# Half of the first columns' products from x times the scale, with the norm and the shift put on the sums

## The chip, the core and the metric

The kernel runs on one NeuronCore of a Trainium2 chip. The metric is the device time of one execution, in microseconds. TensorE (PE in the profile; PEld is its weight load) multiplies, VectorE (DVE) and ScalarE (ACT) work elementwise, GpSimd (POOL) does a few small things, and SyncE (SP) issues the DMAs. Every engine runs its own instructions in the order in which they were written into its queue, and waits on semaphores for the others.

## The reference, cut to what matters

One layer of a diffusion backbone: 1024 tokens of width 1024, 256 context tokens, eight heads of 64, and a gated short convolution beside the attention.

```python
shift, scale, gate = adaln(c, w_ada, b_ada)            # silu(c) @ w_ada + b_ada
h  = rmsnorm(x, norm_g) * (1 + scale) + shift
hc = rmsnorm(ctx, norm_g) * (1 + scale_c) + shift_c
q, k, v, za, u, bg, cg, zc = split(h @ w_in)
kc, vc = split(hc @ w_in[:, 512:1536])
attn = neighbourhood_attention(q, k, v, kc, vc, rpb) * silu(za)
conv = bg * conv3(cg * u) * silu(zc)
x_new = x + gate * (concat(attn, conv) @ w_out)
```

For one feature k and one token t, h is x[t,k] * r[t] * s[k] + b[k]: r is the token's reciprocal root mean square, s is norm_g * (1 + scale), b the shift. So h @ w = r[t] * sum_k (x[t,k] s[k]) w[k] + sum_k b[k] w[k]. The first term without r needs no root mean square, and the second is one number for each column of w.

## The kernel before, in words

Everything is computed with features on the 128 partitions and tokens along the free axis: h lies transposed, as eight k tiles of 128 features by 1024 tokens. For fp32 accuracy each operand is split into a high part (fp32r) and the rest, and each product is three matmuls: high by high, high by low, low by high. `hh[k]` and `hl[k]` are the two parts of h; "half 0" and "half 1" are tokens 0 to 511 and 512 to 1023.

**The first stage** loads everything that h needs and, while that arrives, already multiplies h by the first 384 columns of the convolution (128 columns each of u, bg, cg). Its order is written out by hand: `LOADS` and `STEPS` are lists of words, and `do` runs for each word the function that `does` names. A word writes its instructions into its engine's queue, so the order of the words is the order on each engine. The words, with k the feature tile and h the half:

- `xN`: load the token tile N of x (128 tokens, 512 KB); `thk`: load half h of the transposed x, tile k (256 KB); `sk`: load the slab of the modulation weights for k (1 MB); `ck`, `qk`: a chunk of 384 weight columns (192 KB), for the convolution and for the first projection pair; `n0`, `n1`: context tiles; `e`: transposed context; `g`: the rotary tables.
- `sqN`: ACT squares and sums a token tile; `rootG`: DVE adds epsilon and POOL takes the power -0.5, for a group of tiles (0 and 1 are the halves, 2 is the context); `RtG`: PE turns and spreads the result over the partitions, into a bank `tr`; `RG`: ACT copies it to `spread_r`.
- `prk`: PE multiplies the conditioning vector by slab k (64 small matmuls, into a bank `tr`); `tpk`: DVE turns the rows; `abk`: DVE makes s[k] and b[k] from them.
- `uhk`: DVE makes x * s * r; `hihk`: ACT adds b and writes the high part; `lohk`: DVE writes the low part.
- `chk`, `clk` (and `qhk`, `qlk`): the weight chunk's high part on ACT and the low part on DVE.
- `fchki`: three matmuls, one for each of u, cg, bg, of part i (0 high by high, 1 the low weights, 2 the low h), into the six banks `acc0[column][half]`.
- `TN`, `v0k`: for half 0 and k of 0 and 1, PE turns x itself and DVE normalizes it; `warm`, `fill`: matmuls that only keep PE busy.
- `conv0`: one step of the convolution's first group (`conv_group(0, done)`): copies the sums of u, multiplies by the sums of cg. The taps and the product with bg follow behind the list.
- `rgN`: DVE makes the rotary tables.

**PSUM** has eight banks. In this stage six are `acc0` and two `tr`. Behind it two pools take the eight: `psm` with tags O, U and C, `pss` with tag S, two banks each. A tile of a new pool waits until the old tiles in its bank have been read.

**The second stage** runs over n = 0 to 31: four head pairs by eight token tiles. `proj_tile` multiplies 128 tokens of h by 384 columns (24 matmuls) into a bank whose tag goes round by t % 4. At n = 0, behind the first tile's products, `CONTEXT` makes the context's h (`Hi`, `Lo`: DVE scales, ACT adds the shift and rounds, DVE takes the rest). At n = 2 `ctx_products` multiplies it, 32 matmuls, which PE does in order behind tile 2. Each tile is then normalized by head, rotated, turned and stored; `head_scale` and `normed` read its bank. Beside that stand the convolution's gate unit, sums of blocks of the output weights (`add_blocks`, n = 6 to 25) and **the gate row**: `gate.load(kt)` loads 512 KB of weights, `gate.add(kt)` does two DVE additions a tile, `split` and `sum` end it; the result is loaded into `ab[:, :, 0]`, which the end of the kernel multiplies by.

The third stage is the attention with more units of products as filler, the fourth the output projection.

Of the kernel before, what the change touches and what calls it, by code (L numbers as in the profile page):

```python
# [34 lines left out]

LOADS = "x0 x1 x2 x3 s0 c0 s1 c1 x4 x5 x6 x7 t10 t11 s2 t02 t12 c2"
STEPS = [
# [11 lines left out]
]  # L49
# [6 lines left out]
def body(tc, es, x, xb, xt, cb_, ct, w_mod, w_gate, b_ada, w_grp, w_col, q_g, k_g, bias, w_out, vecs, cst, out):  # L56
# [352 lines left out]
    def conv_group(i, done=None):  # L409
# [6 lines left out]
        def keep(half, ps):  # L416
            ub[half] = cvp.tile([P, 512], F32, name="ub", tag="ub", bufs=2)
            act.copy(ub[half], ps)

# [122 lines left out]
    wpp = wps.enter_context(sbuf("wpp"))  # L542
    cxp = wps.enter_context(sbuf("cxp"))
    xs = ExitStack()
    xp = xs.enter_context(sbuf("xp"))
# [4 lines left out]
    def tr():  # L550
        return ps0.tile([P, 512], F32, name="tr", tag="tr", bufs=2)

# [3 lines left out]
    def load_x(t):  # L556
        if t < 4:
            if t % 2 == 0:
                pair.append(place(6 + t // 2, [P, 2, D], F32, "xn"))
            xn[t] = pair[t // 2][:, t % 2]  # L560
        else:
            xn[t] = xp.tile([P, D], F32, name="xn", tag="xn", bufs=4)[:]
        sp.dma_start(xn[t], xb[t * P:(t + 1) * P] if t < NB else cb_[(t - NB) * P:(t - NB + 1) * P])

    def load_t(half, k):
        xh[half, k] = xp.tile([P, 512], F32, name="xh", tag="xh", bufs=6)
        sp.dma_start(xh[half, k], xt[k, :, half * 512:(half + 1) * 512])
# [10 lines left out]
    for u, half in (0, 0), (2, 0), (0, 1), (2, 1), (1, 0), (1, 1):  # L578
        acc0[u][half] = ps0.tile([P, 512], F32, name=f"acc{u}{half}", tag=f"acc{u}{half}")

    sums = [xp.tile([P, 4], F32, name=f"sums{i}") for i in range(3)]
    spread_r = [xp.tile([P, 512], F32, name=f"rs{i}") for i in range(2)] + [cxp.tile([P, L], F32, name="rs2")]

    def square(t):

        sqj = xp.tile([P, D], BF16, name="sqj", tag="sqj", bufs=1)
        act.activation(sqj, xn[t], AF.Square, scale=1.0 / 32, accum_out=sums[t // 4][:, t % 4:t % 4 + 1])

# [41 lines left out]
    def early(k):  # L630
        return acc0[(0, 2)[k]][1]

# [10 lines left out]
    def scale_early(k):  # L643

        hw = bmp.tile([P, 3 * 384], F32, name="hw", tag="bt", bufs=2)
        scaled[0, k] = hw[:, :512]
        dve.tensor_scalar(scaled[0, k], scaled["v", k], ab[:, k, 1:2], ab[:, k, 0:1], ALU.mult, ALU.add)

    def shift_high(key, hi, k, w):
        if ("v", k) in scaled and key == (0, k):  # L650
            act.activation(hi, scaled["v", k], AF.Identity, bias=ab[:, k, 0:1], scale=ab[:, k, 1:2])
            return
        act.activation(hi, scaled[key], AF.Identity, bias=ab[:, k, 2 * w:2 * w + 1])

    def shift_low(key, lo, hi, k, w):
        if ("v", k) in scaled and key == (0, k):
            scaled.pop(("v", k))
            dve.tensor_tensor(lo, scaled.pop(key), hi.bitcast(F32), ALU.subtract)
            return
        dve.scalar_tensor_tensor(lo, scaled.pop(key), ab[:, k, 2 * w:2 * w + 1], hi.bitcast(F32), ALU.add, ALU.subtract)  # L660

    def half_of(v, half):
        return v[:, half * 512:(half + 1) * 512]

    def first_columns(half, k, i):

        wh, wl = chunks[k][:2]
        for u in (0, 2, 1):
            uc = slice(u * P, (u + 1) * P)
            pe.matmul(acc0[u][half], (wl if i == 1 else wh)[:, uc], half_of(hl[k] if i == 2 else hh[k], half),  # L670
                      start=k == 0 and i == 0, stop=k == KT - 1 and i == 2)

    def cast_chunk(raws, k):
        raw = raws[k][:].rearrange("p a b -> p (a b)")
        w = wpp.tile([P, 2, 384], F32R, name="w", tag="w", bufs=12)
        act.copy(w[:, 0], raw)
        raws[k] = raw, w

    def rest_of_chunk(raws, k):
        raw, w = raws[k]  # L680
        dve.tensor_tensor(w[:, 1], raw, w[:, 0].bitcast(F32), ALU.subtract)
        raws[k] = w[:, 0], w[:, 1], w[:, :, P:384]

# [15 lines left out]
    def gains(i):  # L699

        rw, gqk = tables[0]
        if i == 0:
# [6 lines left out]
        if i == 3:  # L709
            sp.dma_start(rope_d, tables[1][:].rearrange("p n b k d -> p (n b k d)"))  # L710
# [13 lines left out]
    def keep_clock(n, late=False):  # L724

        v = zeros[:].rearrange("p (o n) -> p o n", o=1).broadcast_to([P, 4, P]) if late else warm
        ps = acc0[1][1][:].rearrange("p (a n) -> p a n", a=4) if late else acc0[1][1]
        for _ in range(n):
            pe.matmul(ps, zeros if late else warm[:, :P], v, start=True, stop=True)
# [7 lines left out]
        "Rt": lambda g: copies.update({g: spread_rows(g)}), "R": lambda g: copies[g](),  # L737
        "pr": lambda k: products(k), "tp": lambda k: turned_rows(k), "ab": lambda k: modulation(k),
        "ch": lambda k: cast_chunk(chunks, k), "cl": lambda k: rest_of_chunk(chunks, k),
# [52 lines left out]
    def bank(name, tag):  # L792
        return (pss if tag == "S" else psm).tile([P, 512], F32, name=name, tag=tag, bufs=2)
# [357 lines left out]
    for n in range(NT + 3):  # L1151
# [21 lines left out]
        if 6 <= n < 26 and blocks[1] == 0:  # L1173
            load_blocks(blocks[0])
        if n == 16:
            sp.dma_start(ab[:, :, 0], g_d.rearrange("o (t p) -> p (o t)", p=P))
# [424 lines left out]
```

## Time and profile before

| | us |
|---|---|
| median of 3 runs (lowest, highest) | 587.03 (586.88, 587.1) |
| the profiled execution | 587.34 |
| its span, first to last instruction | 585.6 |
| PE busy in it | 577.2 (99%) |
| DVE busy in it | 438.6 (75%) |
| ACT busy in it | 282.0 (48%) |

The time of an execution is a little more than the span, since it also holds what lies around the instructions. A row of the timeline gives start, length, engine, line, operation, the tile written and those read, shapes, and xcount where instructions of one kind were merged; in brackets stands the engine's idle time before it and what ended it. Nearly all lines are L71, the helper that records the instructions in order, so the tiles' names tell the places: `acc` are the first columns' sums, `pacc` a projection tile, `cacc` the context products, `h` the parts of h, `hw` the scaled x before them, `hc` the context's h, `w` weight chunks, `rs` the spread roots, `rg` rotary tables, `cu` and `cv` the convolution, `gacc` the gate row.

### The profile page before, as it was taken

To read this page: it belongs to the slowest core of one execution; us is meant where nothing else is said; L and a number is where in the kernel's file an instruction comes from. 1 tells how busy PE (TensorE), PEld (TensorE's weight loads), DVE (VectorE), ACT (ScalarE), POOL (GpSimd) and SP (SyncE) were. 2 spreads that over 40 slices of the span, in tenths; PEclk is the share of its full clock that TensorE was granted. 3 is DMA by queue.
4 is the path that set the end of the run, shared out by engine and by line. 5 is a ranking of instruction groups with operands and counts; after the bars stand their busy time and mean duration, and the time that the engine had idled before them with its cause. 6 is when DMAs were issued, how large, how long until landed. Compare 5 with 4: busy or idle time off the path is not lost.

```text
span 585.6 us, 9903 instructions
## 1 busy us (share of the span) xinstructions
PE 577.2 (99%) x3531; PEld 483.3 (83%) x3532; DVE 438.6 (75%) x890; ACT 282.0 (48%) x653; POOL 57.4 (10%) x82
## 2 busy tenths in 40 slices
PE   8899999999999999999999999999999999999997
PEld 4578999999999999988878787878787867888886
DVE  1578879656846746367998788998979887999952
ACT  5636355336525545433463474466535646643420
POOL 1001033123223232100000000000000001100000
PEclk9999999999999999999999999999999999999999
DMA  8997666845756695686253646564758273773532
GB/s 323 410 415 278 220 229 211 283 166 194 267 189 213 224 341 205 226 297 219 73 209 120 243 140 229 182 216 155 254 187 257 80 263 96 248 252 89 199 125 91
DMA packets 66679, 126.14 MB, mean 215 GB/s; under 512 B 8714, under 2 KB 27650, under 8 KB 64325
## 3 DMA queue, kind: packets, MB, share of 16 engines
q1 hardware_dynamic: 66244, 124.70, 60.8%
q0 software_dynamic: 384, 0.81, 0.6%
q8 instruction: 28, 0.46, 0.3%
q14 instruction: 23, 0.18, 0.1%
HBM read 92.38 MB, written 33.10 MB: 214 GB/s over the span
## 4 chain that ended last, share of the span: by engine, by line
PE 91%; DMA 5%; DVE 2%; ACT 1%; SPq 0%; issue 0%; POOL 0%; DVEq 0%; ACTq 0%
PE pu L71 29%; PE pacc L71 23%; PE pout L71 13%; PE acc L71 5%; PE po L71 5%; PE cacc L71 4%; PE pss L71 3%; DMA xn<-in_xb 3%; PE pc L71 3%; PE pmx L71 2%; PE trA L71 1%; PE tr L71 1%; DMA y_d<-tb 1%; PE ptot L71 1%; PE trB L71 1%; DVE sb L71 0%
## 5 line engine op out<-in xcount | busy, mean ns | idle before, releaser
L71 PE MATMUL pu<-h,uh 128*128 128x512 f32 x544 | 174.4, 402 | 0.0
L71 PE MATMUL pacc<-w,h 128*128 128x384 f32 x768 | 138.5, 337 | 0.0
L71 PEld LDWEIGHTS pacc<-w,h 128*128 128x128 f32 x768 | 132.8, 188 | 0.2
L71 PEld LDWEIGHTS pu<-h,uh 128*128 128x128 f32 x544 | 97.3, 188 | 18.4 <-issue 1.2
L71 PE MATMUL pu<-h,ul 128*128 128x512 f32 x272 | 106.5, 391 | 0.0
L71 PE MATMUL pout<-right,left 128*128 128x512 f32 (+2 forms) x348 | 77.0, 383 | 0.0
L71 PEld LDWEIGHTS pout<-right,left 128*128 128x128 f32 x348 | 64.4, 188 | 12.7
L71 PEld LDWEIGHTS pu<-h,ul 128*128 128x128 f32 x272 | 51.1, 188 | 11.5
L71 POOL TENSOR_TENSOR ss<-ss,few 128x4 f32<-128x4 f32 (+1 forms) x40 | 41.4, 1035 | 127.0 <-DVE ss L71 126.7
L71 ACT COPY sc<-pc 128x512 f32<-128x512 f32 x32 | 18.7, 587 | 44.6 <-PE pc L71 44.6
L71 PE MATMUL acc<-h,w 128*128 128x512 f32 x144 | 35.3, 397 | 1.4 <-ACT h L71 1.4
L71 ACT ACTIVATE sc<-sc 128x512 f32<-128x512 f32 x32 | 20.3, 633 | 33.7 <-DVE sc L71 33.6
L71 ACT ACTIVATE sq<-pacc 128x256 f32<-128x256 f32 x32 | 12.3, 386 | 47.4 <-PE pacc L71 46.7
L71 DVE TENSOR_TENSOR sum<-sum,sb 128x372 f32<-128x372 f32 (+2 forms) x64 | 31.1, 485 | 2.7
L71 PEld LDWEIGHTS acc<-h,w 128*128 128x128 f32 x144 | 26.3, 188 | 7.8 <-ACT h L71 2.1
L71 DVE SCALAR_TENSOR_TENSOR m<-pout,ab,m 128x512 f32<-128x512 f32 (+2 forms) x34 | 22.9, 717 | 13.0 <-PE pout L71 12.9
L71 ACT ACTIVATE qn<-pacc,ss 128x64 f32<-128x64 f32 x128 | 30.0, 330 | 4.8 <-PE trA L71 2.5
L71 DVE TENSOR_TENSOR mx<-mx,sb 128x372 f32<-128x372 f32 (+2 forms) x64 | 30.8, 481 | 1.4
L71 DVE TENSOR_REDUCE ss<-sq 128x4 f32<-128x260 f32 (+1 forms) x40 | 15.7, 393 | 21.5 <-ACT sq L71 21.5
L71 DVE TENSOR_TENSOR ul<-uraw,uh 128x512 fp32r<-128x512 f32 x34 | 23.1, 685 | 10.0 <-ACT uh L71 10.0
L71 DVE TENSOR_TENSOR sb<-pss,bt 128x192 f32<-128x192 f32 (+3 forms) x48 | 27.5, 600 | 2.3 <-PE pss L71 2.2
L71 DVE TENSOR_TENSOR qs<-trA,qs 128x512 fp32r<-128x512 f32 x16 | 11.1, 691 | 21.2 <-ACT qs L71 20.2
(142 smaller groups left out, 862.8 us busy)
## 6 DMA issues: line engine op xcount, KB each, us to landing
uraw<-in_w_col SPq DMA_DIRECT2D x34, 256.0 KB, 3.8
slab<-in_w_mod SPq DMA_DIRECT2D x8, 1024.0 KB, 9.0
q_d<-qs SPq DMA_DIRECT2D x32, 256.0 KB, 4.0
k_s<-k_d SPq DMA_DIRECT2D x8, 1024.0 KB, 6.9
q_s<-q_d SPq DMA_DIRECT2D x16, 512.0 KB, 3.9
wr<-in_w_grp SPq DMA_DIRECT2D x40, 192.0 KB, 5.0
bt<-in_rpb SPq DMA_DIRECT2D x8, 564.0 KB, 6.8
xn<-in_xb SPq DMA_DIRECT2D x8, 512.0 KB
```

The source lines that it names most:

```text
L71: i = emit(*a, **kw)
```

## The change

Half 1's first columns no longer take the true h. Word `p1k` (ACT) writes the high part of x * s, `m1k` (DVE) the low part, both into half 1 of `hh[k]` and `hl[k]`; the `fc1ki` multiply these. The shift goes through PE on its own: `shk` (ACT, in place of DVE's second operation in `ab`) writes b[k] into a table `b32` of 32 columns, `wbk` multiplies it by the raw weight chunk (four fp32 matmuls of 96 columns, in the four column groups of a new bank `shifted`), and `wt` (DVE) turns the sum. Behind the last product `rp0` to `rp2` (DVE) multiply the three banks of half 1 by the spread roots, and in `conv_group` ACT adds the shift's column to each of the three, one of them in the copy that was there. The true h of half 1, which the projection tiles from t = 4 on read, is made afterwards by the same `u1k`, `hi1k`, `lo1k`, over the plain parts.

The words stand in a new order: slabs and transposed x of half 1 come first, token tiles of x later; the `fc` words begin with half 1. `tr` has one bank in place of two, the buffers of token tiles go from four to two, those of the transposed x from six shared to three and eight. `proj_tile`'s tags go S, S, O, O. The gate row's loads, additions and sum, and the load of the result, come eight tiles later.

```diff
-LOADS = "x0 x1 x2 x3 s0 c0 s1 c1 x4 x5 x6 x7 t10 t11 s2 t02 t12 c2"
+LOADS = "s0 t10 c0 x0 s1 t11 c1 x2 x3 x1 s2 c2 t12 t02"
 STEPS = [
...
+    "ch0 pr0 s3 t13 c3 t03 t14 c4 t04 tp0 ab0 p10 cl0 sh0 sq0 fc101 fc100 m10 fc102 pr1 s4 x4 x5 T0 ch1 wb0 tp1",
+    "ab1 cl1 p11 sh1 m11 fill2 fc110 sq2 sq3 fc111 fc112 sq1 root0 wb1 T3 ch2 T2 fill5 pr2 s5 tp2 ab2 cl2 sh2 p12",
+    "m12 T1 more Rt0 wb2 R0 fc120 fc121 v00 fc122 hi00 v01 u00 hi01 pr3 lo00 u01 lo01 u02 t05 t15 c5 fc000 fc002",
+    "fc010 tp3 hi02 ab3 fc001 ch3 fc012 p13 fc011 lo02 cl3 fc020 sh3 u03 fc022 hi03 ch4 fc021 m13 fc132 pr4 cl4",
+    "tp4 fc131 sq4 x6 ab4 lo03 fc130 u04 sh4 p14 fc031 fc140 sq5 x7 t16 s6 c6 t06 s7 t17 c7 t07 hi04 fc032 lo04",
+    "ch5 fc141 sq6 fc030 cl5 pr5 fc042 tp5 fc041 fc040 sh5 ab5 wb3 q0 p15 u05 fc151 hi05 sq7 m14 ch6 fc050 root1",
+    "fc150 lo05 m15 fc142 cl6 pr6 tp6 ab6 fc152 sh6 p16 u06 wb5 wb4 q1 q2 g0 n0 n1 m16 hi06 fc051 fc052 ch7 lo06",
+    "pr7 fc162 qh0 qh1 cl7 tp7 fc160 ql0 ab7 qh2 Rt1 fc161 ql1 p17 u07 sh7 wb6 q3 R1 hi07 ql2 u10 fc060 sq8 fc171",
+    "wb7 q4 q5 q7 q6 e0 e1 e2 e3 lo07 u11 fc062 hi10 m17 fc061 fc072 qh3 fc170 sq9 wt ql3 fc071 lo10 qh4 fc172",
+    "hi11 u12 ql4 rp0 root2 qh5 fc070 qh6 ql6 qh7 ql5 ql7 hi12 lo12 lo11 conv0 rp1 u13 u14 hi13 hi14 rg3 lo13 u15",
+    "lo14 hi15 u16 rg0 lo15 rp2 u17 rg2 rg1 hi17 conv0 lo17 Rt2 hi16 R2 lo16",
...
-        ps = bank("pacc", "OOSS"[t % 4])
+        ps = bank("pacc", "SSOO"[t % 4])
...
+            if done and half:
+                act.activation(ub[half], ps, AF.Identity, bias=wbT[:, 0:1])
+                for n, u in enumerate((CBG, CCG)):
+                    act.activation(done[u][1], done[u][1], AF.Identity, bias=wbT[:, 32 * n + 32:32 * n + 33])
+            else:
+                act.copy(ub[half], ps)
...
-        return ps0.tile([P, 512], F32, name="tr", tag="tr", bufs=2)
+        return ps0.tile([P, 512], F32, name="tr", tag="tr", bufs=1)
...
-        dve.tensor_scalar(a[:, 0], rows[k][:, 0:2], bsh[:, k:k + 1], None, ALU.add)
+
+    def shift(k):
+        act.activation(b32[:, k, 0:2], rows[k][:, 0:2], AF.Identity, bias=bsh[:, k:k + 1])
+
+    def shift_products(k):
+
+        raw = chunks[k][2][:].rearrange("p u (g c) -> p u g c", g=4)
+        for g in range(4):
+            pe.matmul(shifted[32 * g:32 * g + 32, :96].rearrange("p (u c) -> p u c", u=3), b32[:, k], raw[:, :, g],
+                      start=k == 0, stop=k == KT - 1, skip_group_check=True)
+
+    def turned_shifts():
+        dve.transpose(wbT, shifted[:, :96])
+
+    def plain_high(k):
+        act.activation(half_of(hh[k], 1), xh[1, k], AF.Identity, scale=ab[:, k, 1:2])
+
+    def plain_low(k):
+        dve.scalar_tensor_tensor(half_of(hl[k], 1), xh[1, k], ab[:, k, 1:2], half_of(hh[k], 1).bitcast(F32),
+                                 ALU.mult, ALU.subtract)
+
+    def normed_bank(u):
+        dve.tensor_tensor(acc0[u][1], acc0[u][1], spread_r[1], ALU.mult)
...
-        if 1 <= n <= KT:
-            gate.load(n - 1)
+        if 9 <= n <= KT + 8:
+            gate.load(n - 9)
...
-        if 2 <= n < KT + 2:
-            gate.add(n - 2)
+        if 10 <= n < KT + 10:
+            gate.add(n - 10)
...
-        if n == KT + 3:
+        if n == KT + 11:
             gate.split()
-        if n == KT + 5:
+        if n == KT + 13:
             gate.sum()
```

More of the change, by code (lines that the diff above doesn't have):

```diff
@@ L417, in keep @@
             ub[half] = cvp.tile([P, 512], F32, name="ub", tag="ub", bufs=2)
-            act.copy(ub[half], ps)
+            if done and half:
[4 more added lines that the diff above has]
+                act.copy(ub[half], ps)
         def multiplied(half, ps):
@@ L543, in body @@
     cxp = wps.enter_context(sbuf("cxp"))
+    wbT = cxp.tile([P, 96], F32, name="wbT")
+    b32 = cxp.tile([P, KT, 32], F32, name="b32")
+    pool.memset(b32, 0.0)
     xs = ExitStack()
@@ L561, in load_x @@
         else:
-            xn[t] = xp.tile([P, D], F32, name="xn", tag="xn", bufs=4)[:]
+            xn[t] = xp.tile([P, D], F32, name="xn", tag="xn", bufs=2)[:]
         sp.dma_start(xn[t], xb[t * P:(t + 1) * P] if t < NB else cb_[(t - NB) * P:(t - NB + 1) * P])
     def load_t(half, k):
-        xh[half, k] = xp.tile([P, 512], F32, name="xh", tag="xh", bufs=6)
+        xh[half, k] = xp.tile([P, 512], F32, name="xh", tag=("xh", "xi")[half], bufs=(3, 8)[half])
         sp.dma_start(xh[half, k], xt[k, :, half * 512:(half + 1) * 512])
@@ L579, in body @@
         acc0[u][half] = ps0.tile([P, 512], F32, name=f"acc{u}{half}", tag=f"acc{u}{half}")
+    shifted = ps0.tile([P, 512], F32, name="shifted", tag="shifted")
     sums = [xp.tile([P, 4], F32, name=f"sums{i}") for i in range(3)]
@@ L584, in square @@
     def square(t):
-        sqj = xp.tile([P, D], BF16, name="sqj", tag="sqj", bufs=1)
-        act.activation(sqj, xn[t], AF.Square, scale=1.0 / 32, accum_out=sums[t // 4][:, t % 4:t % 4 + 1])
+        sqj = cvp.tile([P, T + 2], F32, name="sqj", tag="cu", bufs=1) if t < 4 else xn[t]
+        act.activation(sqj[:, :D], xn[t], AF.Square, scale=1.0 / 32, accum_out=sums[t // 4][:, t % 4:t % 4 + 1])
     def root(g):
@@ L630, in early @@
     def early(k):
-        return acc0[(0, 2)[k]][1]
+        return acc0[(0, 2)[k]][0]
     def transposed(t):
@@ L646, in scale_early @@
         scaled[0, k] = hw[:, :512]
-        dve.tensor_scalar(scaled[0, k], scaled["v", k], ab[:, k, 1:2], ab[:, k, 0:1], ALU.mult, ALU.add)
+        dve.tensor_scalar(scaled[0, k], scaled["v", k], ab[:, k, 1:2], b32[:, k, 0:1], ALU.mult, ALU.add)
     def shift_high(key, hi, k, w):
         if ("v", k) in scaled and key == (0, k):
-            act.activation(hi, scaled["v", k], AF.Identity, bias=ab[:, k, 0:1], scale=ab[:, k, 1:2])
+            act.activation(hi, scaled["v", k], AF.Identity, bias=b32[:, k, 0:1], scale=ab[:, k, 1:2])
             return
-        act.activation(hi, scaled[key], AF.Identity, bias=ab[:, k, 2 * w:2 * w + 1])
+        act.activation(hi, scaled[key], AF.Identity, bias=b32[:, k, w:w + 1])
     def shift_low(key, lo, hi, k, w):
@@ L659, in shift_low @@
             return
-        dve.scalar_tensor_tensor(lo, scaled.pop(key), ab[:, k, 2 * w:2 * w + 1], hi.bitcast(F32), ALU.add, ALU.subtract)
+        dve.scalar_tensor_tensor(lo, scaled.pop(key), b32[:, k, w:w + 1], hi.bitcast(F32), ALU.add, ALU.subtract)
     def half_of(v, half):
         return v[:, half * 512:(half + 1) * 512]
+    done = [0, 0]
     def first_columns(half, k, i):
-        wh, wl = chunks[k][:2]
+        raw, w = chunks[k][:2]
+        wh, wl = w[:, 0], w[:, 1]
         for u in (0, 2, 1):
@@ L670, in first_columns @@
             pe.matmul(acc0[u][half], (wl if i == 1 else wh)[:, uc], half_of(hl[k] if i == 2 else hh[k], half),
-                      start=k == 0 and i == 0, stop=k == KT - 1 and i == 2)
+                      start=done[half] == 0, stop=done[half] == 3 * KT - 1)
+        done[half] += 1
     def cast_chunk(raws, k):
@@ L676, in cast_chunk @@
         act.copy(w[:, 0], raw)
-        raws[k] = raw, w
+        raws[k] = raw, w, raws[k]
     def rest_of_chunk(raws, k):
-        raw, w = raws[k]
+        raw, w = raws[k][:2]
         dve.tensor_tensor(w[:, 1], raw, w[:, 0].bitcast(F32), ALU.subtract)
-        raws[k] = w[:, 0], w[:, 1], w[:, :, P:384]
+        if raws is ch:
+            ch[k] = w[:, 0], w[:, 1], w[:, :, P:384]
     ch = {}
@@ L701, in gains @@
         rw, gqk = tables[0]
-        if i == 0:
+        if len(tables) == 1:
             pool.tensor_scalar(gqk[:, 0], gqk[:, 0], 0.125, None, ALU.mult)
@@ L708, in gains @@
         dve.tensor_tensor(tables[1][:, n, :, k], rraw, gqk[:, k:k + 1].broadcast_to([P, NB, HD]), ALU.mult)
-        if i == 3:
+        tables.append(i)
+        if len(tables) == 6:
             sp.dma_start(rope_d, tables[1][:].rearrange("p n b k d -> p (n b k d)"))
@@ L726, in keep_clock @@
         v = zeros[:].rearrange("p (o n) -> p o n", o=1).broadcast_to([P, 4, P]) if late else warm
-        ps = acc0[1][1][:].rearrange("p (a n) -> p a n", a=4) if late else acc0[1][1]
+        ps = acc0[1][0][:].rearrange("p (a n) -> p a n", a=4) if late else acc0[1][0]
         for _ in range(n):
@@ L737, in body @@
         "Rt": lambda g: copies.update({g: spread_rows(g)}), "R": lambda g: copies[g](),
-        "pr": lambda k: products(k), "tp": lambda k: turned_rows(k), "ab": lambda k: modulation(k),
+        "pr": lambda k: products(k), "tp": lambda k: turned_rows(k), "ab": lambda k: modulation(k), "sh": lambda k: shift(k),
+        "wb": lambda k: shift_products(k), "wt": lambda: turned_shifts(), "p": lambda h, k: plain_high(k),
+        "m": lambda h, k: plain_low(k), "rp": lambda u: normed_bank(u),
         "ch": lambda k: cast_chunk(chunks, k), "cl": lambda k: rest_of_chunk(chunks, k),
@@ L1174, in body @@
             load_blocks(blocks[0])
-        if n == 16:
+        if n == 24:
             sp.dma_start(ab[:, :, 0], g_d.rearrange("o (t p) -> p (o t)", p=P))
```

11 rows, old and new, of the table STEPS are left out of this document.

## The prediction

> **What bounds the kernel now.** I read the page first, then busy time by stretches, the chain of waits up to 100 us, and the timeline of that stretch. The page's busy times:
>
> ```profile
> PE 577.2 (99%) x3531; PEld 483.3 (83%) x3532; DVE 438.6 (75%) x890; ACT 282.0 (48%) x653; POOL 57.4 (10%) x82
> ```
>
> Busy time by stretches (start:end, length, then PE, PEld, DVE, ACT, POOL; last the granted clock, DMA share, GB/s):
>
> ```profile
> 0.00:20.00 20.00, 16.91 (x191) 9.35 (x193) 6.40 (x17) 12.48 (x21) 2.27 (x11) 1.00 0.89 347
> 20.00:40.00 20.00, 18.13 (x257) 13.19 (x256) 12.91 (x28) 9.49 (x18) 1.02 (x1) 1.00 1.03 412
> 40.00:60.00 20.00, 20.00 (x266) 16.04 (x265) 15.57 (x32) 11.11 (x22) 2.10 (x6) 1.00 0.79 294
> 60.00:70.00 10.00, 10.00 (x55) 9.46 (x55) 8.53 (x15) 3.79 (x7) 0.52 (x1) 1.00 0.64 229
> 70.00:80.00 10.00, 10.00 (x59) 9.47 (x58) 8.38 (x20) 5.64 (x14) 1.05 (x2) 1.00 0.74 263
> 80.00:100.00 20.00, 20.00 (x117) 19.28 (x116) 17.51 (x44) 11.06 (x44) 9.63 (x10) 1.00 0.59 185
> 100.00:120.00 20.00, 20.00 (x109) 18.36 (x109) 11.95 (x27) 7.23 (x24) 2.46 (x2) 1.00 0.75 249
> 120.00:140.00 20.00, 20.00 (x119) 19.34 (x118) 12.75 (x31) 8.93 (x34) 4.86 (x5) 1.00 0.72 242
> 584.80:585.60 0.80, 0.00 (x0) 0.00 (x0) 0.00 (x0) 0.00 (x0) 0.00 (x0) 0.50 0.00 0
> ```
>
> PE is never idle between 40 and 140, so a microsecond won or lost before it starts its uninterrupted run is one in the total. And DVE is at 78 to 88% from 40 to 100: it is the engine with the least room. The chain (start, length, what):
>
> ```profile
> 3.08 6.35 DMA xn<-in_xb
> 9.45 12.32 DMA xn<-in_xb
> ...
> 23.29 1.03 POOL sums L71
> ...
> 31.80 5.03 PE acc L71 x21
> 36.83 1.03 PE tr L71 x64
> ...
> 58.38 4.78 PE acc L71 x21
> 63.16 12.50 PE pacc L71 x72
> 75.66 5.55 PE cacc L71 x32
> 81.21 8.32 PE pacc L71 x48
> ```
>
> Up to 21.77 the chain is the loads of x: half 1's root mean square waits for the eighth x tile. From 31.80 it is PE alone: 114 first-column matmuls and four slabs' products ("pr", 1.03 each) up to 63.16, so (31.36 - 4.12) / 114 = 0.239 us a matmul. Three projection tiles take 12.50, the context products 5.55. The prices of the other engines, from the timeline (start, length, engine, xcount):
>
> ```profile
> 1.52 2.74 PE L71 MATMUL acc<-warm 128*128 128x512 bf16 x6 [1.52 <-POOL warm L71]
> 4.48 3.20 PE L71 MATMUL acc<-warm 128*128 128x512 bf16 x14
> 13.41 1.29 DVE L71 TENSOR_TENSOR hw<-acc,rs 128x512 f32<-128x512 f32 x2 [2.55 <-ACT rs L71]
> 29.46 1.41 DVE L71 SCALAR_TENSOR_TENSOR hw<-xh,ab,rs 128x512 f32<-128x512 f32 x2
> 30.24 1.39 ACT L71 ACTIVATE h<-hw,ab 128x512 fp32r<-128x512 f32 x2 [2.00 <-DVE hw L71]
> 31.00 1.42 DVE L71 SCALAR_TENSOR_TENSOR h<-hw,ab,h 128x512 fp32r<-128x512 f32 x2
> 38.22 0.29 DVE L71 TENSOR_SCALAR ab<-rw,b,vecT 128x2 f32<-128x2 f32 x1
> 38.41 0.22 DVE L71 TENSOR_SCALAR ab<-rw,vecT 128x2 f32<-128x2 f32 x1
> ...
> 60.70 0.59 ACT L71 COPY ub<-acc 128x512 f32<-128x512 f32 x1 [0.23 <-PE acc L71]
> 61.32 0.69 DVE L71 TENSOR_TENSOR cu<-acc,ub 128x512 f32<-128x512 f32 x1 [1.56 <-ACT ub L71]
> 61.93 1.49 DVE L71 TENSOR_TENSOR w<-wr,w 128x384 fp32r<-128x384 f32 x3
> 63.30 0.38 ACT L71 COPY rs<-tr 128x256 f32<-128x256 f32 x1
> 64.04 1.88 DVE L71 TENSOR_TENSOR rg<-rw 128x512 f32<-128x512 f32 x3
> 66.31 3.05 DVE L71 SCALAR_TENSOR_TENSOR cv<-cu,vecT,cv 128x512 f32<-128x512 f32 x4
> 69.28 1.28 DVE L71 TENSOR_TENSOR cv<-acc,cv 128x512 f32<-128x512 f32 x2
> 70.47 0.87 DVE L71 SCALAR_TENSOR_TENSOR hw<-xc,ab,rs 128x256 f32<-128x256 f32 x2
> 77.10 0.88 DVE L71 SCALAR_TENSOR_TENSOR hc<-hw,ab,hc 128x256 fp32r<-128x256 f32 x2 [0.18 <-ACT hc L71]
> 80.83 0.93 ACT L71 ACTIVATE qn<-pacc,ss 128x64 f32<-128x64 f32 x4 [0.89 <-POOL ss L71]
> 83.00 1.41 DVE L71 SCALAR_TENSOR_TENSOR gacc<-gs,c,gacc 128x512 f32<-128x512 f32 x2
> ```
>
> Each engine keeps the written order. DVE ends the conv taps at 70.5, then makes the context's h until 77.98 (7.5 us); PE comes to the context products at 75.66, having waited for nothing.
>
> **The change, PE's side.** DMA is full (412 GB/s) until about 50 us, so order in the queue decides. x3, behind 2.19 MB (sizes from the tiles' shapes), lands at 9.43; x7, behind 6.78 MB, at 21.77. At about 0.405 MB/us between these and after, s0 (1.14 MB now) lands near 6.8, s2 (6.25 MB) near 19.4, s7 (17.2 MB) near 46.4. So pr0 runs at 7.8, right behind the 14 warm matmuls, and half 1 begins near 10.3 instead of 27.2; but k=2 waits for s2. From 19.4: pr2 1.03, its rows turned and the multiplier 0.6, the plain high part 0.7, waits between engines 0.3: "fc120" at 22.0, with 6 of the 48 "fc" words (three matmuls each) done. From there PE has work without a gap: 42 words x 0.717 = 30.1, five pr 5.15, Rt1 and the shift products 1.05: 58.3. The true end waits for "root2", written behind "rp0" on DVE: last half-1 product 57.5, then 0.65 + 0.17, POOL 1.03 and the transposes: the first projection tile starts at **59.9 instead of 63.16, 3.3 us earlier**. Added in the same way, the old word list comes to 63.0, so I trust this to half a microsecond.
>
> The 32 shift products have no row. Below: the pr row, 64 matmuls of 64 columns in 1.03, gives 0.1 us for four of 96 columns. Above: a 512-column matmul's 0.24 each, so 0.96 for four, 5 us more in all behind fc120. They have pr's shape (32 columns out, four column groups), so I take 0.12.
>
> **The change, DVE's side.** It loses eight additions of 0.22 (now "sh" on ACT, which had idle time there). It gains eight "m" of 0.71 and three "rp" of 0.65. What matters more is when: u1k and lo1k (1.41 a pair) were spread between PE's steps and come now nearly all behind the last pr. pr7 ends at 22.0 + 30 fc words (21.5) + 5.15 + 0.36 = 49.0, and DVE has tp7 0.25, ab7 0.29, three ql 1.5, u07, u10, lo07, u11 and m17 (3.5) up to m17: 54.7. Behind m17 the list still holds:
>
> - u12 to u17, 6 x 0.705 = 4.2; lo10 to lo17, 8 x 0.71 = 5.7
> - rp0 to rp2, 1.95; ql3 to ql7, 2.6; four rg, 2.5
> - two conv products, 1.4; wt and root2's addition, 0.4
>
> That is 18.75 us, and 1.7 of waits (the second conv product waits for three ACT passes over the sums): 75.2. Then taps and products 3.05 + 1.28 = 4.3, to 79.5, and the context's 7.5, to **87.1, where the trace has 77.98**.
>
> **Where the paths meet.** Tile 1 now takes the second "S" bank. Banks follow first use, so S lies on "shifted" and "tr"; "tr" is free after R2, which ACT has behind hi17, the sums' three passes and hi16. u17 ends at 70.4; 0.7 + 3 x 0.59 + 0.7 + 0.38 gives R2 at 74.1. PE ends tile 0 at 64.1 and **stands 10 us**, with everything behind it. Then tiles 1 and 2 (8.34) and the context products (5.55): 88.0; the last context h, at 87.1, comes in time.
>
> After such a gap the first matmuls are slow. At the start six warm matmuls took 2.74 us where fourteen took 3.20, so 1.37 is lost until the array is warm; and the last stretch shows the clock at 0.50 some 2 us behind the last matmul. So 1.4 more: 89.4 against 81.21, **+8.2 us**.
>
> The Trainium skill ("TensorE: Matmul & The Clock Gate", Part 1) says that an idle window of about 3.4 us puts the clock back to half and a busy one of that length restores it. By that rule 3.4 us at half speed would lose 1.7, and the trace's 0.50 behind the last matmul agrees.
>
> Later waits: tile 4 needs tile 0's bank, whose last reader (qn) ended 3.8 us behind the context's h; 90.9 then, with tile 4 due at 93.6. Half 1's true h is there at 75. Nothing that I see is late after that; PE's later work is the same, so nothing is won back either.
>
> **Gate rows** take 16 additions, 11.3 us of DVE by the 1.41 row, and 4 MB of loads from tiles 1 to 9 to tiles 9 to 17. In 100 to 140 DVE is free for 15.3 us, so they fit; behind each load in SP's queue stand q, k and v stores and weight chunks, as before. I cost them at nothing; without that cover, 1.41 a tile. Their leaving helps DVE only behind the context's h, where PE's loss is already made.
>
> **Sum.** Profiled execution: span 585.6, 587.34 with what lies around it. 587.34 + 8.2 = 595.5; the runs' median is 0.3 below the profiled one, so **595.3**.
>
> **Rivals.**
>
> - *Tile 1 doesn't wait for R2* (another bank, or R2 early). Then the context's h alone decides: 87.1 + 0.7 for the last step, 87.8, +6.6: 593.6. For it: DVE's list is enough by itself. Against: the order of the banks.
> - *PE's side is later*: the transfers slip 1 to 2 us (x7's own landing lay 0.8 behind my rate), or the shift products cost up to their upper bound. DVE's list hangs on pr7, so all slips along: 597 to 600.
> - *The early start wins.* The queue behind m17 is the place: if DVE got through it so that R2 is done at 64.1 and the last context h at 77.9, nine us earlier than I find, the 3.3 us would stay: 584.0. It needs the second pass over half 1 done while DVE waits for PE between 22 and 43. For it: DVE is busy there only 13 of 20 us in the old trace. Against: the written order keeps u10 behind ab7, and ops of 0.7 us don't shrink. It decides as soon as DVE is less than 3 us behind the old times.
> - *It cancels*: 5 us of stall instead of 10; 587 plus or minus 1.
>
> **How the numbers follow.** Forecast 0.48, tile 1 free 0.17, PE later 0.17, early start 0.13, cancels 0.05. The range goes from below the second case to the far end of the third, 591 to 600; it leaves out the two last. 0.2% (1.2 us) is about what a measurement of this kernel can tell from no change: faster 0.14, same 0.04, slower 0.82.
>
> **What would show it.** First acc matmul on half 1 near 10; the first pacc matmul near 60; a PE gap of some 10 us behind 24 pacc matmuls, ended by ACT's rs copy; granted clock below 1.00 in it; DVE without a pause from 43 to 87; context products ending near 89. Wrong: no such gap, or DVE's conv taps over before 72; then the forecast falls with it. If the gap is there but ended by DVE's hc, the first rival holds.

## The result and the profile after

The changed kernel takes **603.03 us** in the median of 4 runs (602.64 to 603.68), beside 587.07 (586.88 to 588.14) for the kernel before on the same chip: a ratio of 1.0269, 95% interval 1.0251 to 1.0287. It is slower, as forecast, but 7.7 us beyond the forecast and 3 beyond the end of its range. The profiled execution is the 602.64 one; its span is 600.8 (585.6 before), so 15.2 us are to be found. In the run "R2 early" below one of the four executions, the profiled one, took 725.27 us at a granted clock of 0.75 and is left out.

First the stretches, with the columns of the prediction (start:end, length, then PE, PEld, DVE, ACT, POOL; granted clock, DMA share, GB/s):

```profile
60.00:70.00 10.00, 5.28 (x22) 4.67 (x21) 7.88 (x15) 6.53 (x14) 2.06 (x6) 0.83 0.45 169
70.00:80.00 10.00, 2.42 (x15) 2.10 (x13) 8.64 (x14) 5.42 (x10) 0.00 (x0) 0.82 0.15 66
...
160.00:180.00 20.00, 19.05 (x115) 18.62 (x114) 19.55 (x45) 9.81 (x35) 4.47 (x4) 1.00 0.86 285
```

The last of them in the kernel before:

```profile
160.00:180.00 20.00, 20.00 (x122) 19.31 (x121) 8.47 (x23) 6.80 (x26) 5.35 (x6) 1.00 0.46 153
```

PE, full from 40 to 140 before, stands for 12.3 us between 60 and 80, at a lowered clock around it, and loses another 0.95 between 160 and 180, where DVE is full (19.55 of 20, and 8.47 before). The chain of waits (start, length, what) shows what ended last:

```profile
23.05 2.33 PE acc L71 x9
...
43.45 0.30 PE shifted L71 x8
...
48.62 0.51 PE shifted L71 x16
...
52.13 7.63 DMA xn<-in_cb
...
79.66 0.27 ACT rs L71
79.98 10.06 PE pacc L71 x48
90.04 5.55 PE cacc L71 x32
```

And the timeline (start, length, engine, operation, tiles, shapes, xcount, in brackets the idle time before it and what ended it):

```profile
26.89 0.22 PE L71 MATMUL tr<-slab,c 128*32 128x64 f32 x1 [0.48 <-issue]
...
50.60 1.10 PE L71 MATMUL tr<-slab,c 128*32 128x64 f32 x64
56.53 5.06 PE L71 MATMUL acc<-h,w 128*128 128x512 f32 x21
57.53 0.75 DVE L71 SCALAR_TENSOR_TENSOR h<-xh,ab,h 128x512 fp32r<-128x512 f32 x1
59.79 1.06 ACT L71 ACTIVATE xn<-xn 128x1024 f32<-128x1024 f32 x1 [3.71 <-DMA xn<-in_cb]
62.08 0.56 DVE L71 TENSOR_TENSOR w<-wr,w 128x384 fp32r<-128x384 f32 x1 [3.62 <-ACT w L71]
66.30 0.69 PE L71 MATMUL tr<-ci,sums 128*128 128x128 f32 x2 [4.72 <-POOL sums L71]
66.64 5.75 PE L71 MATMUL pacc<-w,h 128*128 128x384 f32 x24
79.98 10.06 PE L71 MATMUL pacc<-w,h 128*128 128x384 f32 x48 [7.58 <-ACT rs L71]
91.72 0.88 DVE L71 SCALAR_TENSOR_TENSOR hc<-hw,b,hc 128x256 fp32r<-128x256 f32 x2 [0.18 <-ACT hc L71]
174.10 2.21 PE L71 MATMUL pacc<-w,h 128*128 128x384 f32 x11 [0.95 <-DVE w L71]
```

In the kernel before ACT squared the first context tile nearly 13 us earlier, without a wait:

```profile
47.03 1.05 ACT L71 ACTIVATE sqj<-xn 128x1024 bf16<-128x1024 f32 x1
```

The context products (`cacc`) end at 95.59 where they ended at 81.21: 14.4 us. With the 0.95 at 174 that is the span's 15.2, within 0.2. The large gap is the one forecast: PE stands behind 24 `pacc` matmuls until ACT's `rs` copy (R2). That copy ended at 79.9, not at 74.1. The first gap, 4.72 us ahead of `tr<-ci,sums`, costs nothing by itself here, since tile 1 waits for R2 in either case.

### The profile page after: what moved, and what is told of

It is laid out like the page before. It is cut to its first block, busy times and chain, and to the rows that moved or that the text cites. A ratio compares the mean times of both kernels' runs of the same rounds, so it can differ in the third digit from the quotient of the medians.

```text
span 600.8 us, 10008 instructions
## 1 busy us (share of the span) xinstructions
PE 579.1 (96%) x3574; PEld 484.9 (81%) x3574; DVE 445.8 (74%) x894; ACT 290.2 (48%) x671; POOL 58.0 (10%) x83
## 4 chain that ended last, share of the span: by engine, by line
PE 82%; DMA 8%; DVE 6%; ACT 2%; SPq 1%; issue 1%; DVEq 0%; ACTq 0%
PE pu L71 27%; PE pacc L71 19%; PE pout L71 13%; PE po L71 5%; PE cacc L71 4%; PE acc L71 3%; PE pss L71 3%; PE pc L71 2%; DMA slab<-in_w_mod 2%; PE pmx L71 2%; DMA xn<-in_cb 1%; PE trA L71 1%; DMA wr<-in_w_grp 1%; PE tr L71 1%; DMA y_d<-tb 1%
## 5 line engine op out<-in xcount | busy, mean ns | idle before, releaser
L71 PE MATMUL pacc<-w,h 128*128 128x384 f32 x768 | 141.9, 342 | 8.5 <-ACT rs L71 7.6
L71 PEld LDWEIGHTS pacc<-w,h 128*128 128x128 f32 x768 | 135.5, 192 | 9.3 <-ACT rs L71 7.9
L71 ACT ACTIVATE sq<-pacc 128x256 f32<-128x256 f32 x32 | 12.3, 385 | 48.7 <-PE pacc L71 48.2
L71 ACT ACTIVATE sc<-sc 128x512 f32<-128x512 f32 x32 | 20.3, 633 | 30.0 <-DVE sc L71 29.8
L71 DVE TENSOR_TENSOR sb<-sb,mg 128x744 f32<-128x744 f32 (+2 forms) x32 | 26.7, 834 | 0.0
```

What stands on the lines that cost most here:

```text
L71: i = emit(*a, **kw)
```

## The experiments

The theory was the forecast's mechanism with new sizes: DVE and ACT come to R2 5.8 us later than I found, 3.6 of it there already at m17 and 2.2 left of a wait for the first context tile. The rivals are named with each run. All times stand beside runs of the kernel before on the same chip (587.07 to 587.66 in the median). Executions of one and the same variant of the changed kernel differ by 0.9 to 3.8 us among themselves, so single microseconds are read with that in mind.

**R2 early.**

```diff
-... hi12 lo12 lo11 conv0 rp1 u13 ... hi17 conv0 lo17 Rt2 hi16 R2 lo16
+... qh5 fc070 Rt2 qh6 ... hi12 lo12 lo11 conv0 R2 rp1 u13 ... hi17 conv0 lo17 hi16 lo16
```

> The changed kernel with the copy R2 moved on ACT from behind hi16 to behind the first conv0 step; nothing else. Theory (two locks in a row: the bank of R2 first, DVE's list up to the context's h behind it): tile 1 starts behind tile 0 at about 72, the gap moves to the context products, which now wait for DVE's context h, whose end stays near 92.5; they end near 93.2 in place of 95.6, so 600.6. Rival (the bank alone made the stall): tiles 1 and 2 and the context products run through without a gap, 595 or less.

Measured: 602.29 (602.15 to 603.08, three runs), ratio 1.0258 (1.0241 to 1.0275). That is 1.7 above the theory and far from the rival: only 0.7 is won. By the theory the gap does not go away with its cause: the context products, in order behind tiles 1 and 2, wait for the context's h in its place. No profile of this run shows that; one with the same edit stands below, at the run that joins it with the next one.

**The tables' load last.** Word `g0`, two broadcast loads of 32 KB and one of 512 KB, stood ahead of the context tiles `n0` and `n1` in SP's queue; it goes behind the weight chunks.

```diff
-"... q1 q2 g0 n0 n1 m16 ..."
-"wb7 q4 q5 q7 q6 e0 e1 ..."
+"... q1 q2 n0 n1 m16 ..."
+"wb7 q4 q5 q7 q6 g0 e0 e1 ..."
```

> The changed kernel with one word moved: the load of the rotary tables (g0) goes behind the last weight chunk, so that the two context tiles are issued ahead of it. Theory (ACT stood 3.7 us for context tile n0, with qh3 to qh7 and hi10 queued behind it, and DVE stood with it): the wait goes, everything on DVE and ACT up to R2 comes 2.5 to 3.6 us earlier, 599.4 to 600.5. Rival (the chunks q3 to q7, which land just as late, hold ACT in its place): 602.5 to 603.

Measured: 601.06 (598.86 to 602.61), ratio 1.0231 (1.0198 to 1.0264): 2.0 less in the median, half a microsecond short of the theory, with a wide scatter: two executions are at 598.9 and 599.5, and two at 602.6, where next to nothing is won. The profile is of the 599.53 one. Its timeline and chain:

```profile
56.29 1.05 ACT L71 ACTIVATE xn<-xn 128x1024 f32<-128x1024 f32 x1
...
76.17 0.27 ACT rs L71
```

ACT no longer waits ahead of the context tile, and R2 ends 3.5 us earlier in this execution. Why that tile was late shows in the stretches of the changed kernel:

```profile
52.00:53.00 1.00, 1.00 (x6) 0.82 (x5) 0.06 (x1) 0.27 (x1) 0.00 (x0) 1.00 0.25 75
53.00:54.00 1.00, 1.00 (x8) 0.85 (x7) 0.73 (x3) 1.00 (x3) 0.00 (x0) 1.00 0.14 27
54.00:55.00 1.00, 1.00 (x12) 0.47 (x11) 1.00 (x3) 1.00 (x4) 0.00 (x0) 1.00 0.35 92
```

and in SP's queue, by its timeline:

```profile
49.84 0.42 SPq L71 DMA_DIRECT2D rw<-in_q_norm_g  x1
...
52.13 1.23 SPq L71 DMA_DIRECT2D xn<-in_cb  x2
```

The DMA engines are nearly idle from 52 to 55, though the context tiles were issued by 53.4. The tables' load stands ahead of them, the first of its two small broadcast loads at 49.84. That SP came to it no sooner has a cause of its own, which the run with fewer shift products shows.

**PE kept warm.** Thirty matmuls of zeros into a bank that is free then, ahead of tile 1.

```diff
+        if n == 1:
+            spare = psm.tile([P, 512], F32, name="spare", tag="O", bufs=2)
+            v = zeros[:].rearrange("p (o n) -> p o n", o=1).broadcast_to([P, 4, P])
+            for _ in range(30):
+                pe.matmul(spare[:].rearrange("p (a n) -> p a n", a=4), zeros, v, start=True, stop=True)
```

> The changed kernel with 30 matmuls of zeros (0.23 us each) into a free bank between tiles 0 and 1, where PE stands. Theory (the 48 projection matmuls behind the gap took 10.06 us where 48 take 8.32, because the clock had dropped): they take 8.35 to 8.5, so 601.3. Rival (they are slow for another reason, or the filler's own end is late): 603 or more.

Measured: 602.49 (601.36 to 604.49), ratio 1.0251 (1.0232 to 1.027): no difference that can be told. Its chain:

```profile
82.67 8.59 PE pacc L71 x48
```

The 48 matmuls take 8.59 instead of 10.06, so the clock term (1.4 in my sum) is confirmed in size. But in this execution PE came to them 2.7 us later, more than the 1.5 won. The zeros were not the cause, for they ended at 81.8 and R2 at 82.6.

**Gate rows back** at their old tiles, in the changed kernel.

```diff
-        if 9 <= n <= KT + 8:
-            gate.load(n - 9)
+        if 1 <= n <= KT:
+            gate.load(n - 1)
...
-        if 10 <= n < KT + 10:
-            gate.add(n - 10)
+        if 2 <= n < KT + 2:
+            gate.add(n - 2)
```

> The changed kernel with the gate rows back at their old tiles. Theory (moved, their additions meet the weight blocks' sums on DVE at 160 to 180, where PE lost 0.95 us; at the old place DVE has room now): that loss goes and none comes in its place, 602.1. Rival (the move paid for itself, DVE's backlog behind the context's h would hold banks): 603 to 606.

Measured: 603.72 (603.22 to 605.7), ratio 1.0285 (1.0263 to 1.0307), a number in the rival's range. The loss at 174 is gone:

```profile
160.00:180.00 20.00, 20.00 (x121) 19.30 (x120) 14.77 (x37) 11.88 (x41) 5.27 (x5) 1.00 0.71 235
```

but the time is not lower; R2 came at 81.9 in the profiled execution, 2 us later than in the changed kernel's. R2 stands ahead of the gate rows in every queue, and behind the context's h PE waits for nothing up to 200, so the rival's reason isn't seen either. In the changed kernel this run doesn't price the move.

**The gate rows alone**, in the kernel before: the same lines moved the other way.

> The kernel before with nothing but the gate rows eight tiles later. Theory (in the late place their 16 additions fill DVE where the weight blocks are added too, and a weight chunk is late for PE): 1 us slower, 588.0. Rival of the prediction's own step (costs nothing there): 587.1.

Measured: 588.76 (588.54 to 589.39, 8 runs) beside 587.44, ratio 1.0024 (1.0013 to 1.0034). This part alone costs 1.3 us. Its timeline, and a stretch:

```profile
160.35 2.21 PE L71 MATMUL pacc<-w,h 128*128 128x384 f32 x11 [1.44 <-DVE w L71]
```

```profile
140.00:160.00 20.00, 18.91 (x114) 18.50 (x113) 18.98 (x43) 11.49 (x43) 6.45 (x6) 1.00 0.82 272
```

DVE is full at 140 to 160, where the additions now meet the sums of weight blocks; there PE waits for a weight chunk's low part.

**No second pass.** The words u1k, hi1k and lo1k are left out: half 1's true h is never made, and the projection tiles from 4 on multiply x times the scale in its place.

```diff
-... u10 ... u11 ... hi10 ... lo10 ... hi11 u12 ... hi12 lo12 lo11 ... u13 u14 hi13 hi14 ... hi16 R2 lo16
+... R2
```

> The changed kernel without the second pass over half 1: the words u1k, hi1k and lo1k are left out, so the projection of half 1's tokens is computed from the plain parts (x times the scale, without root mean square and shift). Theory (DVE's list behind the last slab products sets the end of the stage): DVE loses 16 operations, some 10 us of them behind m17; R2 comes near 70, the context's h near 82.5, the context products end near 84 in place of 95.6, so 591 to 592.5. Rival (ACT's wait for the context tiles, or the loads, set it): 598 or more.

Measured: 594.43 (593.51 to 596.0), ratio 1.0123 (1.0105 to 1.0141): 8.6 us less, though 2 above the theory. So the second pass, 16 DVE operations of about 0.7 us and eight on ACT, is more than half of the loss, and what is left isn't DVE's list: DVE stands 4.9 us ahead of 64.5 in it. The timeline:

```profile
61.70 1.06 ACT L71 ACTIVATE xn<-xn 128x1024 f32<-128x1024 f32 x1 [3.73 <-DMA xn<-in_cb]
...
68.28 0.69 PE L71 MATMUL tr<-ci,sums 128*128 128x128 f32 x2 [4.59 <-POOL sums L71]
68.62 14.88 PE L71 MATMUL pacc<-w,h 128*128 128x384 f32 x72
```

Tiles 0 to 2 now follow without a gap, but they start at 69.0 where they started at 63.16: "Rt2" stands ahead of tile 0 on PE and needs the context's squares. Their first tile landed at 61.7, and the second one's squares stand on ACT behind the copy of a weight chunk that landed at 63.95. That and the lowered clock (14.54 for the 72 matmuls in the chain, against 12.50) are 7.8 of the 8.6 us by which the span of this execution, 594.2, is above 585.6; the rest is the 0.85 that PE lost at 160 to 180. In the median the run is 7.0 above the kernel before.

**R2 early and the tables last, together.**

> R2 early and the rotary tables' load last, together in the changed kernel. Theory (two locks in a row, and a wait ahead of both): less than either alone suggests is left to the bank; PE runs tiles 0 to 2 without a gap and waits ahead of the context products for DVE's context h, which ends near 89; they end near 90, so 597 to 598.5. Rival (the bank alone): 592 or less; (the gap moves and nothing else): 600 to 601.

Measured: 598.38 (597.67 to 599.01), ratio 1.0183 (1.0168 to 1.0199): 4.7 us less than the changed kernel, where the parts gave 0.7 and 2.0. This fits waits in a row, where each part alone leaves standing what the other takes away. The chain and the timeline:

```profile
81.10 1.95 DVE cv L71 x3
...
83.48 0.52 ACT hc L71
```

```profile
64.43 12.77 PE L71 MATMUL pacc<-w,h 128*128 128x384 f32 x72
84.04 7.98 PE L71 MATMUL cacc<-w,hc 128*128 128x512 f32 x32 [6.84 <-ACT hc L71]
```

This is the forecast's rival "tile 1 doesn't wait for R2" as it really looks: tiles 0 to 2 run at once, and the whole wait stands ahead of the context products, for the first context h. It comes behind the second pass and the conv's taps on DVE.

**m and the tables on POOL**, on top of the last run: each low part as two POOL operations, the four rg there too.

```diff
-        dve.scalar_tensor_tensor(half_of(hl[k], 1), xh[1, k], ab[:, k, 1:2], half_of(hh[k], 1).bitcast(F32),
-                                 ALU.mult, ALU.subtract)
+        pool.tensor_scalar(plain, xh[1, k], ab[:, k, 1:2], None, ALU.mult)
+        pool.tensor_tensor(half_of(hl[k], 1), plain, half_of(hh[k], 1).bitcast(F32), ALU.subtract)
...
-        dve.tensor_tensor(tables[1][:, n, :, k], rraw, ...)
+        pool.tensor_tensor(tables[1][:, n, :, k], rraw, ...)
```

> R2 early, the tables' load last, and 12 DVE operations given to POOL: the eight low parts m1k (two POOL operations each, over a scratch tile) and the four rotary products. Theory (DVE's sum sets the stage): DVE loses 8 x 0.71 + 4 x 0.63 = 8.2 us, of which those of the time behind the last slab products count whole, 3 to 5 us less than R2 and tables alone: 592 to 595. Rival (POOL's slower operations come late for the fc1k2 products, PE stands earlier): as slow as the changed kernel or slower, 603 or more.

Measured: 606.88 (605.63 to 607.45), ratio 1.0329 (1.0315 to 1.0343); the rival holds, and in this profile PE stands 4.1 us in all for the low parts. The timeline of POOL, and of DVE below it:

```profile
65.10 1.56 POOL L71 TENSOR_SCALAR plain<-xh,ab 128x512 f32<-128x512 f32 x1 [8.03 <-DMA rw<-in_q_norm_g]
66.75 1.26 POOL L71 TENSOR_TENSOR h<-plain,h 128x512 fp32r<-128x512 f32 x1
```

```profile
64.19 0.75 DVE L71 SCALAR_TENSOR_TENSOR h<-hw,b,h 128x512 fp32r<-128x512 f32 x1
```

Two POOL operations take 2.8 us and more where one of DVE took 0.75, and m17 stood 8 us before its first. The view names the load of the gains there, but m17 doesn't read it, and the gains' own work on POOL comes later, at 71.04. The likelier releaser is DVE's lo10, which ended at 64.94: m17's scratch tile shares two buffers with half 1's scaled x, which lo10 reads.

**Fewer shift products**: six of the eight words wb left out, so half 1's shift lacks six of its eight terms.

> The changed kernel without six of the eight words of shift products (wb1 to wb6): half 1's shift lacks six of its eight terms, so 1.8 us of PE's work in the first stage is left out. If the price of the shift products (0.30 us a word where I took 0.12) is on the path, as a term of my sum: 601.0 to 601.5, 1.5 to 2 us less than the changed kernel's 603.0. Rival: ACT's wait for the first context tile, which follows SP's queue and not PE, ends last; then 602.5 to 603.5, no change.

Measured: 601.17 (600.63 to 602.35), ratio 1.0235 (1.0215 to 1.0256): 1.9 less than the changed kernel for 1.8 of PE's work. The number is the theory's, but the path isn't. PE ends pr7 only 1.1 us earlier, while the context tile is squared 2.9 us earlier, and R2 ends as much earlier with it:

```profile
56.88 1.06 ACT L71 ACTIVATE xn<-xn 128x1024 f32<-128x1024 f32 x1 [1.83 <-DMA xn<-in_cb]
```

ACT still waits for that tile, as the rival had it; but the tile doesn't follow SP's queue apart from PE. The waits of SP (what it waited for, us in total, times, longest) in the changed kernel, from 43.8 to 49.9, have this row:

```profile
SPq L71 <- PE shifted L71: 3.0, 1, 3.0
```

In the run with fewer shift products it has none, and the first load of the tables goes out at 46.98 instead of 49.84. A raw weight chunk has one of five buffers, and the shift products are new readers of it: the chunks q1 and q2, ahead of the tables in SP's queue, take the buffers that wb4 and wb5 read. So the words cost PE 0.30 us each, and SP 3.0 us once.

**The context's h first**, on top of "R2 early and the tables last": the words of `CONTEXT` go ahead of u13, and rp2 and the second conv0 ahead of them.

```diff
-... lo12 lo11 conv0 R2 rp1 u13 u14 ... lo15 rp2 u17 rg2 rg1 hi17 conv0 lo17 hi16 lo16
+... lo12 lo11 conv0 R2 rp1 rp2 conv0 Hi0 Hi1 Lo0 Lo1 ... Hi6 Hi7 Lo6 Lo7 u13 u14 ... lo15 u17 rg2 rg1 hi17 lo17 hi16 lo16
...
-            if n == 0:
-                do(CONTEXT)
```

> Root 2's copy early and the tables' load late, as in the run at 598.4, and the context's h made ahead of the larger part of the second pass over half 1 (u13 to u17, lo13 to lo17), which only the projection tiles from tile 4 on read. Theory (the amount of DVE work decides, not its order): tiles 1 and 2 and the context products follow without the 8 us gap and the context products end near 81 to 83 instead of 92; but tile 4 takes tile 0's bank, whose reader on ACT follows DVE's whole list, and that list is as long as before and ends near 87; so PE stands there for some 6 to 8 us instead, and 593 to 595 remains. Rival 1 (the order alone was at fault): no gap of over 1 us anywhere, 588 to 590. Rival 2 (PE waits twice, nothing won): 598.

Measured: 603.97 (603.14 to 604.47), ratio 1.0275 (1.026 to 1.0291). The first half of the theory holds to the microsecond and the second is far off. The timeline of PE and ACT:

```profile
63.30 12.75 PE L71 MATMUL pacc<-w,h 128*128 128x384 f32 x72
75.89 5.71 PE L71 MATMUL cacc<-w,hc 128*128 128x512 f32 x32
...
94.68 1.22 ACT L71 CAST uh<-uraw 128x512 fp32r<-128x512 f32 x2 [8.88 <-DMA uraw<-in_w_col]
...
99.21 5.78 PE L71 MATMUL pacc<-w,h 128*128 128x384 f32 x24 [13.45 <-ACT qn L71]
```

PE runs from 63.3 to 85.8 much as it did from 63.16 in the kernel before, and then stands 13.45 us for tile 0's bank. Behind DVE's list, which ends at 89.6, come 9 us that I had not seen, in the chain:

```profile
87.64 0.76 DVE cv L71
...
88.51 0.96 POOL gacc L71
89.49 0.25 SPq L71
...
89.79 4.79 DMA uraw<-in_w_col
```

The gate row's buffer lies where the conv's `cu` was: POOL's memset waits for the taps, SP's small load for the memset, and the gate unit's weights stand behind that load. ACT needs them ahead of tile 0's squares.

**The same with the gate rows back.**

> The run with the context's h first, with the gate rows also back at their old tiles. Theory: their eight tiles' delay costs 1.3 us, as it did in the kernel before, so 1.3 us less than that run, 592 to 594. Rival: DVE is the late engine at tiles 1 to 9 now, so the 16 additions of 0.7 us there cost more than they save, 1 to 5 us above that run.

Measured: 603.34 (602.44 to 604.35), ratio 1.0267 (1.0248 to 1.0285), 0.6 less; the intervals overlap, and it decides nothing.

**SP's queue free**: the run with the context's h first, rg ahead of the context's words, and the gate row's buffer made at tile 8.

```diff
-... rp2 conv0 Hi0 ... hi14 rg3 lo13 ... u16 rg0 lo15 u17 rg2 rg1 hi17 ...
+... rp2 conv0 rg3 rg0 rg2 rg1 Hi0 ... hi14 lo13 ... u16 lo15 u17 hi17 ...
...
-    gate = gate_row()
...
+        if n == 8:
+            gate = gate_row()
```

> The run with the context's h first, with two things taken out of SP's queue ahead of the loads of the gate unit's weights (uraw): the rotary tables (rg) come ahead of the context's h on DVE, so that their store is out by 70, and the gate row's buffer and its small load, which stand behind the conv's taps by way of POOL's memset, are made at tile 8, just ahead of its first rows. In the run with the context's h first, ACT stood 8.9 us for uraw and so reached tile 0's bank at 95.8, and PE stood 13.4 us for that bank. Theory: uraw lands before 85, ACT and DVE come to tile 0 right behind the conv's taps near 90, tile 4 starts near 92 to 93 instead of 99.2, and 596 to 598 remains. Rival: something else holds tile 0's reader (the order of DVE or ACT alone, or a colder clock), and less than 2 us is won: 602 to 604. Other side: with uraw early nothing waits for the end of DVE's list, 588 to 591.

Measured: 599.38 (598.53 to 599.83), ratio 1.0201 (1.0184 to 1.0218): 4.6 less than the run with the context's h first, 1.4 above the theory's range. The two edits were made together, and they take 5.0 us off the 13.45. The timeline and two stretches:

```profile
93.39 7.22 PE L71 MATMUL pacc<-w,h 128*128 128x384 f32 x24 [8.41 <-ACT qn L71]
```

```profile
89.00:90.00 1.00, 0.00 (x0) 0.00 (x0) 0.29 (x1) 0.96 (x3) 0.00 (x0) 0.63 1.06 395
...
99.00:100.00 1.00, 1.00 (x6) 1.00 (x6) 0.96 (x3) 1.00 (x6) 0.43 (x1) 0.75 0.00 0
```

Tile 4 starts at 93.39, near the 92 to 93 expected, but uraw landed at 89.4 in the chain and not before 85, so its load still holds ACT. And the 24 matmuls take 7.2 us where 4.2 is usual, because the clock stays low for 6 us. Moving DVE's work about moves the wait: from R2, to the context's h, to tile 0's bank. No order that was tried beats the kernel before.

## Why the prediction was wrong

**Right**: the sign, the place, the releaser and the second wait behind it. PE's gap behind 24 `pacc` matmuls, ended by ACT's `rs` (7.6 us, for my 10); the clock below 1.00 around it; half 1's second pass as the largest cause (8.6 us); the context's h as the next wait once R2 is early.

**Wrong, the step "R2 at 74.1".** It was done at 79.9; that 5.8 is nearly all of the 6.2 by which the context products missed my 89.4. With the 0.95 of the gate rows below, it makes the 7.1 us between the profiled execution, 602.64, and my 595.5. By its terms:

- *m17 at 54.7*: it ended at 58.3, 3.6 later. pr7 ended at 51.7 instead of 49.0. Of these 2.7 us, 1.0 was there at "fc120" (23.05 for 22.0), since the slab s2 landed at 20.4 and not at 19.4. The rate was wrong: x3 and x7, the landings I named, lie 4.59 MB and 12.34 us apart, which is 0.372 MB/us and not 0.405, and by 0.372 s2 comes at 20.3. Another 0.7 is pr3, which took 1.72 us for 1.03; PE stood 0.48 ahead of its last matmul there, for nothing that the profile shows. About 0.5 is the 90 first-column matmuls behind fc120 (22.0 for 21.5), and 0.45 the three words of shift products among them (0.81 for 0.36), where I took the lower bound because they resemble "pr" rows. The last 0.9 of the 3.6 came behind pr7: DVE stood 1.21 us ahead of ab7 for ACT's copy of a weight chunk, which ACT had awaited.
- *18.75 us of list and 1.7 of waits behind m17*: DVE alone stood 3.62 us there, behind ACT's 3.71 for the first context tile. My sum has no term for that tile. The list and the other waits came out 1.4 shorter than I summed, so 2.2 of the 3.62 reaches R2. Two things stood ahead of the tile in SP's queue: SP's wait of 3.0 us for the shift products, which I had priced in PE's time alone, and the tables' three loads, behind two of which the DMA engines were nearly idle for 3 us.
- *The clock, 1.4*: 48 matmuls took 10.06 against my 8.34 + 1.4 = 9.74. Right.

**Wrong, "Gate rows ... I cost them at nothing".** I checked 100 to 140, which is not their new place: of the eight pairs of additions two start there when the move is made alone (127.6 and 139.0), and none in the changed kernel, where they run from 141.8 to 182.3. At 160 to 180 DVE was at 19.55 of 20: 0.95 us there, 1.3 when moved alone.

**Wrong, "the first projection tile starts at 59.9".** It started near 67, later than the 63.16 of before. PE was through the first columns at 61.6 and then stood 4.72 us for root2, whose addition DVE makes behind its pause of 3.62. "DVE without a pause from 43 to 87" failed at the same place. This added nothing, since R2 came later still.

**The rivals.** "Tile 1 doesn't wait for R2" was right as a mechanism (PE waits for the context's h) and too low in price: 593.6 against 602.3, or 598.4 with the tables last. "PE's side is later", 597 to 600, named the right terms but not the loads that come on top of them. "The early start wins" asked for DVE less than 3 us behind the old times; its context h ended at 92.6 instead of 77.98. "It cancels" asked for 5 us of stall, and PE stood 12.3.

What stays open: how much of ACT's wait is the tables' loads and how much SP's wait for the shift products, since the run with the tables last and the one with fewer shift products each won about 2 us and shorten the same wait, and no run does both.

## What to carry to other kernels

Work taken off the path by algebra still has to be done: here the true h came back as a second pass on the engine with the least room, ahead of everything that the next stage waits for, so ask what stands behind the added work in that engine's order, buffers and queues. Removing the last wait wins only up to the next one; price that before moving anything. A new reader of a buffer is a new wait for whoever fills that buffer next: products that cost PE 0.3 us a word held the load queue for 3.0. So a load's cost is its place in the queue and what the queue waits for ahead of it, not only its bytes.

## What the runs showed of the hardware

- Two to four microseconds behind the issue of two broadcast loads of 32 KB the DMA share was 0.25, 0.14 and 0.35 (52 to 55 us), with larger loads queued behind them. In the run with R2 early and the tables last, the first was issued at 58.62, and the hole moved with it:

```profile
62.00:63.00 1.00, 1.00 (x6) 0.63 (x4) 1.00 (x3) 1.00 (x3) 0.00 (x0) 1.00 0.05 14
```

  In the run with fewer shift products the hole is shallower (no share under 0.62 from 50 to 55). In the kernel before the first was issued at 43.94, and from 44 to 53 no microsecond is lower than this one:

```profile
50.00:51.00 1.00, 1.00 (x6) 0.84 (x5) 0.94 (x3) 0.99 (x2) 0.88 (x1) 1.00 0.77 275
```

  That these loads block the others fits the places of the holes; why they would in the one place and not in the other isn't shown.
- The granted clock stays at 1.00 through about four microseconds of idle PE (in the last run PE ends at 85.0 and the clock falls within 89 to 90) and then stays at 0.50 until 3.2 to 6.1 us of matmuls have run (from 79.98 to near 83.1 in the changed kernel, from 93.39 to near 99.5 in the last run). In the changed kernel:

```profile
83.00:84.00 1.00, 1.00 (x7) 1.00 (x7) 0.96 (x3) 0.00 (x0) 0.00 (x0) 0.90 0.52 197
```

  So a gap cost 1.7 (10.06 for 8.32) and 3.0 us (7.22 for 4.19) of clock in these two. The Trainium skill ("TensorE: Matmul & The Clock Gate", Part 1) has windows of about 3.4 us that run free, and says that the cost varies from run to run. It does vary in these traces, and 3.2 to 6.1 us would be about one to two such windows; no run here shows the windows themselves.
- Matmuls of fp32 data with 96 columns appear as two instructions each: eight for a word of four products, 0.30 us in the chain.
- POOL took 1.56 us for a 128x512 multiplication by a column and 1.26 for the subtraction in the rows above, where DVE's fused operation took 0.75.
